# Two instead of three pairs of split buffers for the weight tiles of the feed-forwards

## The chip, the cores and the metric

The kernel runs on one core of one Trainium2 chip. The metric is the device time of one execution in microseconds (us). TensorE (PE) multiplies, VectorE (DVE) and ScalarE (ACT) work on tiles in the on-chip memory, GpSimd (POOL) and SyncE (SP) issue DMAs here.

## The reference

One decoder block on x of 256 tokens by 2048, in float32, depth 1:

```python
x = x + 0.5 * swiglu_ffn(rms_norm(x, ffn1_norm), ffn1_w_gate, ffn1_w_up, ffn1_w_down)
z = rms_norm(x, mix_norm) @ w_in                  # 2048 -> 5120
...                                               # conv, gated recurrence, short conv: y
x = x + y @ w_out                                 # 2048 -> 2048
x = x + 0.5 * swiglu_ffn(rms_norm(x, ffn2_norm), ffn2_w_gate, ffn2_w_up, ffn2_w_down)
return rms_norm(x, final_norm)

def swiglu_ffn(x, w_gate, w_up, w_down):          # 2048 -> 5632 -> 2048
    return (jax.nn.silu(x @ w_gate) * (x @ w_up)) @ w_down
```

## The kernel before

Every large product is done with operands split into two parts: `hi` is the value rounded to the type fp32r, and `lo` is what is left of it. A product is then three matmuls: weight `hi` with the activations' `hi`, weight `hi` with the activations' `lo`, weight `lo` with the activations' `hi`. The activations are split once; the weights are split as they arrive. A weight tile is 512 rows by 512 columns (`[128, UK=4, CW=512]`, 8 KB in each partition): SP fetches it into a raw buffer, ACT casts it to `hi` in two halves (`parts_of`, lines 214 to 219), DVE subtracts to get `lo` (`low_part`), and TensorE reads both. One weight tile against one group of 128 tokens is 12 matmuls of 512 columns (8 with `hi`, 4 with `lo`); against both groups, 24.

The buffers for `hi` and `lo` come from `split_tiles` (lines 198 to 206). The pool `splits`, open for the whole program, has two pairs. While `extra` holds a pool, each third weight tile takes its pair from elsewhere: in the mixer (`extra[0] is bigs`) from the pool of large tiles, otherwise from the stage's own pool, with one more pair. `extra` is set by `more_from` in `ffn` (line 526, both feed-forwards), in the mixer's `sc_c` (line 1181) and ahead of the output projection (line 1258). Outside of these, in the mixer's `columns` above all, there are two pairs.

A large part of the work goes through `seven` (lines 417 to 522): two by two blocks of a product done with seven multiplications instead of eight (a Strassen scheme), where some weight tiles are sums of others, formed in place on DVE, or by an accumulating DMA of POOL. Its order for a gate or up block is, by call:

- `product_of(0)` (raw tile w11), then DVE sums w12 into w11
- `product_of(4)` (that sum); ACT copies both results out of the accumulators (`s1`, `s5`)
- `usual(0, b2, 1)`: a plain weight tile against both token groups
- the next sum into w11, `product_of(5)`, copy `u2`
- `usual(1, b3, 1)`; `product_of(6)` (w12 with the DMA's sum), copy `u3`; `product_of(2)`
- `usual(0, a2, 0)`; a third sum; `product_of(3)`; `usual(1, a3, 0)`; `product_of(1)`

A `product_of` is 12 matmuls, a `usual` is 24. `done` adds the copies together with small DVE operations. A feed-forward (`ffn`, lines 524 to 921) begins with one column block done plainly, then has five steps `s`, each a gate block, an up block and, for `s` of 0, 2 and 4, a part of the down projection (`down`): a plain product (`product`), a block of seven, a plain product. `settle` turns finished hidden tiles with TensorE transposes (`ph`), which ACT and DVE split.

The order of the instructions on each engine is not that of the code, except in the opening of the first feed-forward, where `Engine.pinned` keeps it: a list scheduler plans it when the program is built, by its own estimate of when each operand and each buffer is ready. On the chip every engine then keeps to its planned order, and waits on semaphores. Which buffer of a pool a tile gets is decided there too. Almost all instructions have line 43 in the profile, that of the wrapper `Engine`, so groups are told apart by their tiles.

In the profile's names, `hi_g_p`, `hi_u_p`, `hi_d_p` are the tiles of a `product_of` of a gate, up or down block, `hi_g_x` those of a `usual`, `hi_d`, `hi_in` and so on those of a plain product; `ps_u_a` is the accumulator `a` of an up block, `z`, `s_g`, `s_u`, `u_g` are small result tiles.

Of the kernel before, what the change touches and what calls it, by code (L numbers as in the profile page):

```python
# [49 lines left out]
def hybrid_block(ctx: ExitStack, tc: tile.TileContext, a: dict, out: bass.AP):  # L50
# [28 lines left out]
    bigs = ctx.enter_context(tc.tile_pool(name="bigs", bufs=10, side="left"))  # L79
# [92 lines left out]
    def big(name):  # L172

        return bigs.tile([P, UK, 2 * S], F32R, tag="big", name=name)
# [3 lines left out]
    extra = []  # L178
# [18 lines left out]

    def split_tiles(name):
        pool, bufs = splits, 2
        if extra:  # L200
            turn_of["split"] += 1
            if turn_of["split"] % 3 == 0:
                if extra[0] is bigs:
                    return [big(f"{part}_{name}") for part in ("hi", "lo")]
                pool, bufs = extra[0], 1
        return [pool.tile([P, UK, CW], F32R, tag=part, name=f"{part}_{name}", bufs=bufs) for part in ("hi", "lo")]
# [7 lines left out]
    def parts_of(raw, name):  # L214
        hi, lo = split_tiles(name)
        for h in (slice(0, 2), slice(2, UK)):
            act.copy(hi[:, h, :], raw[:, h, :])
        low_part(raw, hi, lo)
        return blocks(hi, lo)
# [197 lines left out]
    def seven(w, rows, cols, sf, xs, name, keep, done, between=None, early=False, own=None, factor=None):  # L417
# [51 lines left out]
        if early:  # L469
            between("second product")  # L470
            hi, lo = split_tiles(f"{name}_x01")
            act.copy(hi, b2)
            s1 = snap(a, "s1")
            dve.tensor_tensor(w11, w22, w11, op=ALU.add)
            low_part(b2, hi, lo)
            blk = blocks(hi, lo)
        else:
            s1 = snap(a, "s1")
# [12 lines left out]
        if early:  # L491
            blk = parts_of(b3, f"{name}_x11")
            hi2, lo2 = split_tiles(f"{name}_p2")
            act.copy(hi2, w22)
            blk2 = blocks(hi2, lo2)
# [909 lines left out]
```

## Time and the profile before

| | before |
|---|---|
| median of 3 runs | 1727.16 us (1727.0 to 1728.76) |
| profiled execution | 1726.91 us, its span 1725.1 us |
| granted TensorE clock, mean | 0.999 |
| PE busy | 1715.3 us (99%), 7985 matmuls |
| DVE busy | 1452.2 us (84%) |
| ACT busy | 1077.8 us (62%) |
| fetched from memory | 339.82 MB, 198 GB/s over the span |

The span is the time from the first to the last instruction. A row of the timeline has its start (us), its duration, engine, line, operation, output and inputs, and how many instructions were merged; brackets at the end give the idle time before it and what ended it. A row of the groups has the count, then busy time in us and the mean of one in ns, then the idle time before and its releasers. PE rows of 8 matmuls last 1.98 us because the end of the last overlaps with the next row.

### The profile page before, as it was taken

The numbers are of one execution on the slowest core, as the hardware profiler recorded it, in microseconds if no ns is written. First come the engines' busy times: TensorE is split into PE (matmuls) and PEld (weight loads), VectorE is DVE, ScalarE is ACT, GpSimd is POOL, SyncE is SP. The second block draws the span as 40 slices with busy tenths as digits, with TensorE's granted clock in tenths as the row PEclk, the third lists the DMA queues.
The fourth block names the chain that finished last, engine by engine and source line by source line (L and its number), as shares of the span: only waits on it lengthen the run. The fifth ranks groups of instructions, "written<-read, shape, count | busy, mean of one in ns | idle before, by whom it ended". The sixth has DMA issues, their size and how long they took to land.

```text
span 1725.1 us, 20426 instructions
## 1 busy us (share of the span) xinstructions
PE 1715.3 (99%) x7985; PEld 1432.9 (83%) x7985; DVE 1452.2 (84%) x1212; ACT 1077.8 (62%) x1406; POOL 35.3 (2%) x62
## 2 busy tenths in 40 slices
PE   9999999999999999999999999999999999999998
PEld 8888888888888888888888888888888888888886
DVE  7988889789789888787897889889788887788886
ACT  7666566656466656666965657655556664556664
POOL 0010000000000000000000000000000000000000
PEclk9999999999999999999999999999999999999999
DMA  8775777667677766655556675776777757677753
GB/s 300 225 258 174 242 234 227 214 236 233 182 238 226 227 201 219 211 160 193 175 197 205 204 251 165 228 237 224 230 227 219 244 171 243 214 225 220 254 179 128
DMA packets 178256, 372.59 MB, mean 216 GB/s; under 512 B 6132, under 2 KB 9072, under 8 KB 174448
## 3 DMA queue, kind: packets, MB, share of 16 engines
q1 hardware_dynamic: 173632, 340.81, 58.4%
q0 software_dynamic: 4352, 29.43, 8.5%
q8 instruction: 62, 1.02, 0.2%
q10 hardware_dynamic: 176, 1.06, 0.2%
q14 instruction: 34, 0.28, 0.0%
HBM read 339.82 MB, written 2.10 MB: 198 GB/s over the span
## 4 chain that ended last, share of the span: by engine, by line
PE 99%; DVE 0%; ACT 0%; DVEq 0%; issue 0%; ACTq 0%
PE ps_d L43 14%; PE ps_in L43 10%; PE ps_g_a L43 9%; PE ps_u_a L43 9%; PE ps_g_c L43 6%; PE ps_u_c L43 6%; PE ps_d_a L43 5%; PE ps_u_d L43 5%; PE ps_g_d L43 5%; PE ps_d_c L43 3%; PE ps_u_e L43 3%; PE ps_g_e L43 3%; PE ps_g L43 3%; PE ps_o L43 3%; PE ps_u L43 3%; PE ps_d_d L43 3%
## 5 line engine op out<-in xcount | busy, mean ns | idle before, releaser
L43 ACT CAST hi_g_p<-raw_g 128x1024 fp32r<-128x1024 f32 (+1 forms) x139 | 142.1, 1054 | 111.6 <-DVE raw_g L43 26.9
L43 DVE TENSOR_TENSOR lo_g_p<-raw_g,hi_g_p 128x2048 fp32r<-128x2048 f32 x70 | 159.8, 2289 | 42.3 <-ACT hi_g_p L43 41.6
L43 DVE TENSOR_TENSOR lo_u_p<-raw_u,hi_u_p 128x2048 fp32r<-128x2048 f32 x70 | 159.3, 2288 | 39.5 <-ACT hi_u_p L43 39.2
L43 ACT CAST hi_u_p<-raw_u 128x1024 fp32r<-128x1024 f32 x140 | 141.3, 1047 | 70.1 <-issue 23.1
L43 PE MATMUL ps_d<-hi_d,h 128*128 128x512 f32 x696 | 166.0, 390 | 0.0
L43 PEld LDWEIGHTS ps_d<-hi_d,h 128*128 128x128 f32 x696 | 130.0, 188 | 26.6
L43 ACT CAST hi_d<-raw_d 128x1024 fp32r<-128x1024 f32 x88 | 88.6, 1048 | 68.3 <-PE ps_u_d L43 19.9
L43 DVE TENSOR_TENSOR lo_d<-raw_d,hi_d 128x2048 fp32r<-128x2048 f32 x44 | 100.8, 2290 | 29.3 <-ACT hi_d L43 29.3
L43 PE MATMUL ps_in<-xT_nm,hi_in 128*128 128x512 f32 x512 | 122.5, 391 | 0.0
L43 ACT CAST hi_d_p<-raw_d 128x1024 fp32r<-128x1024 f32 x84 | 85.2, 1048 | 59.2 <-DVE raw_d L43 33.7
L43 PEld LDWEIGHTS ps_in<-xT_nm,hi_in 128*128 128x128 f32 x512 | 94.0, 188 | 18.8 <-ACT tha L43 0.5
L43 DVE TENSOR_TENSOR lo_d_p<-raw_d,hi_d_p 128x2048 fp32r<-128x2048 f32 x42 | 95.5, 2288 | 15.5 <-ACT hi_d_p L43 15.4
L43 ACT CAST hi_g_x<-raw_g 128x1024 fp32r<-128x1024 f32 (+1 forms) x79 | 81.2, 1058 | 42.9 <-PE ps_g_c L43 25.6
L43 ACT CAST hi_u_x<-raw_u 128x1024 fp32r<-128x1024 f32 x80 | 80.5, 1046 | 36.4 <-PE ps_u_c L43 22.1
L43 DVE TENSOR_TENSOR lo_g_x<-raw_g,hi_g_x 128x2048 fp32r<-128x2048 f32 x40 | 91.5, 2288 | 9.2 <-ACT hi_g_x L43 8.9
L43 DVE TENSOR_TENSOR lo_in<-raw_in,hi_in 128x2048 fp32r<-128x2048 f32 x32 | 73.2, 2288 | 26.7 <-ACT hi_in L43 26.3
L43 DVE TENSOR_TENSOR lo_u_x<-raw_u,hi_u_x 128x2048 fp32r<-128x2048 f32 x40 | 91.4, 2286 | 1.4 <-ACT hi_u_x L43 0.8
L43 PE MATMUL ps_d<-lo_d,h 128*128 128x512 f32 x348 | 86.2, 389 | 0.0
L43 ACT CAST hi_in<-raw_in 128x1024 fp32r<-128x1024 f32 x64 | 64.0, 1045 | 24.9 <-PE ps_in L43 15.2
L43 PEld LDWEIGHTS ps_d<-lo_d,h 128*128 128x128 f32 x348 | 65.3, 188 | 13.6
L43 DVE TENSOR_TENSOR raw_u<-raw_u,raw_u 128x2048 f32<-128x2048 f32 x30 | 68.7, 2289 | 8.5 <-DMA raw_u<-in_ffn_w_up_dram 8.1
L43 DVE TENSOR_TENSOR raw_g<-raw_g,raw_g 128x2048 f32<-128x2048 f32 x30 | 68.7, 2289 | 5.7 <-DMA raw_g<-in_ffn_w_gate_dram 5.2
(477 smaller groups left out, 3750.5 us busy)
## 6 DMA issues: line engine op xcount, KB each, us to landing
raw_d<-in_ffn_w_down_dram SPq DMA_DIRECT2D x88, 1024.0 KB, 5.2
raw_u<-in_ffn_w_up_dram SPq DMA_DIRECT2D x87, 1024.0 KB, 5.3
raw_g<-in_ffn_w_gate_dram SPq DMA_DIRECT2D x86, 1024.0 KB, 5.2
raw_in<-in_w_in_dram SPq DMA_DIRECT2D x32, 1024.0 KB, 5.1
raw_g<-raw_g POOLq DMA_DIRECT2D x10, 1024.0 KB, 7.0
raw_u<-raw_u POOLq DMA_DIRECT2D x10, 1024.0 KB, 7.0
raw_in_c<-in_w_in_dram SPq DMA_DIRECT2D x8, 1024.0 KB, 5.3
raw_o<-in_w_out_dram SPq DMA_DIRECT2D x8, 1024.0 KB, 5.2
```

The lines of the kernel that those rows point to most:

```text
L43: ins = getattr(self.engine, name)(*args, **kwargs)
```

## The change

The condition under which `split_tiles` turns to a third pair is narrowed to the mixer's case. In the feed-forwards and in the output projection every weight tile now takes one of the two pairs of `splits`, in turn. The pair of the stage's own pool is not allocated any more, and nothing else takes its place. Arithmetic, loads and their number stay; the scheduler plans the orders anew.

```diff
     def split_tiles(name):
         pool, bufs = splits, 2
-        if extra:
+        if extra and extra[0] is bigs:
             turn_of["split"] += 1
             if turn_of["split"] % 3 == 0:
                 if extra[0] is bigs:
                     return [big(f"{part}_{name}") for part in ("hi", "lo")]
                 pool, bufs = extra[0], 1
         return [pool.tile([P, UK, CW], F32R, tag=part, name=f"{part}_{name}", bufs=bufs) for part in ("hi", "lo")]
```

## The prediction, made before the changed kernel had run

> **What bounds the kernel now.** I read the page first: busy shares and the chain that ended last.
>
> ```profile
> span 1725.1 us, 20426 instructions
> ...
> PE 1715.3 (99%) x7985; PEld 1432.9 (83%) x7985; DVE 1452.2 (84%) x1212; ACT 1077.8 (62%) x1406; POOL 35.3 (2%) x62
> ...
> PE 99%; DVE 0%; ACT 0%; DVEq 0%; issue 0%; ACTq 0%
> ```
>
> TensorE is busy 99% of the span and is the whole chain. Second view, what TensorE waits for: one row that names a split tile.
>
> ```profile
> PE ps_g L43 <- ACT hi_g L43: 0.6, 1, 0.6
> ```
>
> So the splits (ScalarE casts the high part, VectorE subtracts the low part) have always been ready. Nothing can be won: the idle time of TensorE is 1725.1 - 1715.3 = 9.8 us, and its instructions stay the same. Everything turns on whether the splits stay ahead with two pairs. Third view, the groups: what a split costs.
>
> ```profile
> L43 DVE TENSOR_TENSOR lo_u_p<-raw_u,hi_u_p 128x2048 fp32r<-128x2048 f32 x70 | 159.3, 2288 | 39.5 <-ACT hi_u_p L43 39.2
> L43 ACT CAST hi_u_p<-raw_u 128x1024 fp32r<-128x1024 f32 x140 | 141.3, 1047 | 70.1 <-issue 23.1 <-PE ps_u_a L43 22.6 <-DVE raw_u L43 22.0
> 322.00:364.00 42.00, 42.00 (x191) 34.85 (x190) 34.62 (x22) 26.96 (x31) 0.87 (x1) 1.00 0.73 236
> ```
>
> A low part is 2.29 us, a high part two casts of 1.05 us. The last row (busy time by stretch: PE, PEld, DVE, ACT, POOL, granted clock) is an up-projection's seven-product block: VectorE is busy 34.6 of 42 us, so it has capacity; what it may lack is look-ahead.
>
> **One seam, instruction by instruction.** The timeline where a gate block ends and an up block begins, by engine. I name a weight tile after its call: P0 is product_of(0), X01 is usual(0, b2, 1), X10 is usual(1, a3, 0). A P tile has 12 matmuls, an X tile 24. The PE rows are, in order: P3 (2 rows), X10 (4), P1 (2, of which the first is shown), then in the up block P0 (2), P4, X01, P5, X11.
>
> ```profile
> 313.70 1.98 PE L43 MATMUL ps_g_a<-hi_g_p,x 128*128 128x512 f32 x8
> 315.51 1.07 PE L43 MATMUL ps_g_a<-lo_g_p,x 128*128 128x512 f32 x4
> 316.42 1.98 PE L43 MATMUL ps_g_a<-hi_g_x,x 128*128 128x512 f32 x8
> 318.23 1.98 PE L43 MATMUL ps_g_d<-hi_g_x,x 128*128 128x512 f32 x8
> 320.05 1.07 PE L43 MATMUL ps_g_a<-lo_g_x,x 128*128 128x512 f32 x4
> 320.95 1.07 PE L43 MATMUL ps_g_d<-lo_g_x,x 128*128 128x512 f32 x4
> 321.86 1.98 PE L43 MATMUL ps_g_d<-hi_g_p,x 128*128 128x512 f32 x8
> ...
> 324.58 1.98 PE L43 MATMUL ps_u_a<-hi_u_p,x 128*128 128x512 f32 x8
> 326.39 1.07 PE L43 MATMUL ps_u_a<-lo_u_p,x 128*128 128x512 f32 x4
> 327.30 1.98 PE L43 MATMUL ps_u_c<-hi_u_p,xs 128*128 128x512 f32 x8
> ...
> 330.02 1.98 PE L43 MATMUL ps_u_e<-hi_u_x,x 128*128 128x512 f32 x8
> ...
> 335.46 1.98 PE L43 MATMUL ps_u_a<-hi_u_p,xs 128*128 128x512 f32 x8
> ...
> 338.18 1.98 PE L43 MATMUL ps_u_e<-hi_u_x,x 128*128 128x512 f32 x8
> ```
>
> ```profile
> 315.75 2.00 ACT L43 CAST hi_u_p<-raw_u 128x1024 fp32r<-128x1024 f32 x2 [1.63 <-issue]
> 321.15 0.60 ACT L43 ACTIVATE z<-ps_g_a 128x512 f32<-128x512 f32 x1 [3.40 <-PE ps_g_a L43]
> 322.49 2.00 ACT L43 CAST hi_u_p<-raw_u 128x1024 fp32r<-128x1024 f32 x2 [0.74 <-DVE raw_u L43]
> ...
> 327.99 0.58 ACT L43 ACTIVATE s_u<-ps_u_a 128x512 f32<-128x512 f32 x1
> 330.22 0.60 ACT L43 ACTIVATE s_u<-ps_u_c 128x512 f32<-128x512 f32 x1 [1.65 <-PE ps_u_c L43]
> ```
>
> ```profile
> 317.79 2.29 DVE L43 TENSOR_TENSOR lo_u_p<-raw_u,hi_u_p 128x2048 fp32r<-128x2048 f32 x1 [1.34 <-ACT hi_u_p L43]
> 320.11 2.29 DVE L43 TENSOR_TENSOR raw_u<-raw_u,raw_u 128x2048 f32<-128x2048 f32 x1
> 324.52 2.29 DVE L43 TENSOR_TENSOR lo_u_p<-raw_u,hi_u_p 128x2048 fp32r<-128x2048 f32 x1 [2.12 <-ACT hi_u_p L43]
> 326.74 0.68 DVE L43 TENSOR_TENSOR s_g<-ps_g_d,s_g 128x512 f32<-128x512 f32 x1
> ```
>
> Read what starts P0's high part, at 315.75. The profile says "issue", so no wait that it sees; but P3's high part was last read by the matmuls that end where the next PE row begins, at 315.51, and 0.24 us later the cast starts. P3 lies three tiles before P0 (P3, X10, P1, P0): the cast waits for the third pair to come round. The rest hangs on it: P0's low part 317.79, then VectorE forms the sum w11 + w12 in place (320.11), which is P4's raw tile, then P4's high part (322.49 to 324.49) and low part (324.52 to 326.81). TensorE asks for P4 at 327.30: the lead is 2.8 us for the high part.
>
> PE rows give matmuls 0.227 us apart (8 in 1.81 us), and the other latencies: a cast ends at 317.75 and its subtraction starts at 317.79 (0.04); a sum ends at 322.40 and its cast starts at 322.49 (0.09); X10's matmuls into ps_g_a end where the next row begins, 320.95, and z starts 0.20 later. Operations that follow each other on ACT start 0.1 us before the one before them has ended.
>
> **With two pairs, step by step.** Now P0 takes the pair of the tile two before it, X10. I walk on in the same times, with the orders of the changed program. Two things in them differ at this seam: ACT issues z between the two halves of P0's high part, and s_g's and s_u's activations ahead of P4's high part; VectorE adds s_g ahead of the sum.
>
> X10's high part is free at 320.05 + 0.20 = 320.25 and its low part at 321.86 + 0.20 = 322.06. High part of P0: first half 320.25 to 321.3, z to 321.8, second half to 322.8. Low part 322.8 to 325.1. s_g's small add, then the sum from 325.6 to 327.9. ACT has s_u, the copy of the finished P0 product: it can't start before 327.30 + 0.20 and ends at 328.1, and P4's cast stands behind it. First half of P4's high part 328.0 to 329.05. TensorE wanted it at 327.30 and gets it at 329.1: **a wait of 1.8 us where there was none.** From there: the second half ends at 330.0, P4's low part 330.05 to 332.35; the new PE order puts 6 of X01's high matmuls ahead of P4's low ones, which covers this: with X01's first half at 330.95 they run from 331.0 to 332.4, 0.15 us lost. P4's low matmuls end at 333.3; the copy of ps_u_c (0.60 us, the row at 330.22) holds X01's second target until 334.15, where 8 matmuls covered it before and 2 do now: 0.4 us lost. VectorE does X01's low part to 334.6 and the next sum to 336.8; P5's first half is there at 337.95, and TensorE, which has done X01 at 337.75, loses 0.25 us. X11's first half comes at 339.85 and costs 0.1 us. P5's low part (338.9 to 341.2) is again covered by 6 matmuls of X11. At 342.2 TensorE has 10 of X11's 16 high matmuls left; before, it was there at 338.18 + 6 x 0.227 = 339.54. Loss 2.65 us. Later in the block the tiles are longer or need no sum; P3's low part comes just in time behind five small adds (0 to 0.5 us). I take **2.9 us a seam**.
>
> Bounds: at least 0.9 us, if nothing on ACT stands in the way of P0 and P4 (low part at 322.06, sum to 327.1, half a cast later 328.2 against 327.30); at most 4.0 us, with P3's 0.5 and another 0.1 us on each of some six crossings.
>
> Loads: the walk delays the release of raw tiles, so fetches start later. A fetch takes 5.3 us to land:
>
> ```profile
> raw_u<-in_ffn_w_up_dram SPq DMA_DIRECT2D x87, 1024.0 KB, 5.3
> ```
>
> The nearest is w21, fetched after X11's low part (about 343.6, so there at 349) for a sum that VectorE reaches at about 349: just hidden. I take nothing; if the cover fails it is part of the 4.0.
>
> **How many seams.** The bad place is P1, P0, P4 in a row: short tiles, with a sum between the last two. It exists where a block follows a block: all five up blocks of both feed-forwards (10), and gate blocks 2 and 4 (4), which follow up blocks. The changed PE order says the same: in those 14 blocks X01's high matmuls were moved ahead of P4's low ones. In the gate seam 8 transposes stand ahead of P1 and their copies on ACT; the same walk gives about 3. 14 x 2.9 = 41 us.
>
> The other blocks of seven (gate 1 and 3, gate 0, three down blocks, per feed-forward, and the one of the output projection: 13) come after plain products, whose rows are these:
>
> ```profile
> 430.37 21.76 PE ps_d L43 x96
> ```
>
> Each plain tile is 24 matmuls, 5.44 us, against 2.29 us of VectorE: P0's low part can start a whole plain tile ahead of P0, and P4 is in time. Inside, P5, P6, P2 can cost 0 to 1.5 us; I take 0.6, 8 us in all (0 to 20). Plain products, the mixer's columns (which never had the third pair) and the tail: nothing, each tile has 9 us for its low part. The two openings: 0 to 2 us each, I take 1 each.
>
> **Sum.** 41 + 8 + 2 = 51 us. The profiled execution took 1726.9 us (its span 1725.1 and 1.8 around it), 0.25 below the median shown, 1727.16. Predicted 1778.
>
> A rule of the Trainium skill speaks of the first wait. "TensorE: Matmul & The Clock Gate", Part 1, says that TensorE's clock is halved after an idle window of about 3.4 us. By it my longest wait, 1.8 us, is too short, and the sum stays; the profile's granted clock is 1.00 in the stretch quoted above, and no row of it shows what a wait does.
>
> **Rivals.**
>
> *No wait appears (not slower).* Place: P4 of each of the 14 seams. The moved matmuls of the next X tile fill the time, and two pairs are enough. Price 0: 1727. It decides if P0's low part starts 1.8 us sooner than I have it, at 321.0. For it: VectorE has 7 us free in 42. Against: X10's low matmuls are only then being read (320.05 to 321.86). "Trainium Kernel Development and Optimization", Best Practices, asks for double buffering for performance and no more; that is this rival. Chance 0.05, of which faster by chance of the new order 0.02.
>
> *Shorter.* ACT's order doesn't bite and only the 0.9 us and the small waits after it stay, 1.2 a seam, with 5 for the rest: 14 x 1.2 + 5 = 22, 1749. Against: an engine's own order is fixed in the program. Chance 0.12.
>
> *Wider.* Every one of the 27 blocks pays 2.9, since P5, P6, P2 is the same pattern as P1, P0, P4: 27 x 2.9 = 78, 1805. Against: there TensorE comes out of a 24-matmul tile. Chance 0.12.
>
> *The clock falls.* If a wait drops the granted clock to half for as long as one plain tile, each of 14 seams pays 5.44 us more: 1778 + 76 = 1854. No row shows the clock below 1.00. Chance 0.03.
>
> **How the numbers follow.** My forecast has 0.68. The bounds, 14 x 0.9 with nothing else and 14 x 4.0 + 20 + 4, give 1740 to 1807; the range 1750 to 1808 takes the upper bound in, with the wider rival, and leaves out the clock, no wait, and half of the shorter one and the bottom of the bounds: about 0.2. A measurement here can tell about 0.2% (3.5 us). Faster 0.02, same 0.03, slower 0.95.
>
> **What the profile after would show.** Right: TensorE's busy time as before or stretched, with gaps of 1 to 2 us ahead of P4 in the 14 seams; P0's cast starting 0.2 us after X10's high matmuls; a period of 44 us instead of 41 to 42 for an up block; ACT's s_u ahead of P4's cast. Plain products unchanged. The prediction is wrong if the gaps lie mostly elsewhere (P5, P6, the openings), if the granted clock is below 0.99, or if the span grows by less than 13 us or more than 80.

## The result, and the profile after

| | before | after |
|---|---|---|
| median | 1727.85 us (4 runs, 1727.0 to 1728.76) | 1779.31 us (4 runs, 1777.98 to 1779.55) |
| profiled span | 1725.1 us | 1777.6 us |
| granted TensorE clock, mean | 0.999 | 0.999 |

The ratio is 1.0296, with a 95% interval of 1.0278 to 1.0314: the changed kernel is 3% slower. The forecast was 1778.0 us (1750 to 1808). The page of the kernel after (span, busy times, chain that ended last, and one group of the splits):

```profile
span 1777.6 us, 20462 instructions
...
PE 1735.6 (98%) x7985; PEld 1425.6 (80%) x7985; DVE 1451.0 (82%) x1212; ACT 1078.5 (61%) x1406; POOL 35.5 (2%) x62
...
PE 92%; DVE 3%; ACT 3%; issue 1%; DMA 1%; DVEq 0%; ACTq 0%
...
L43 DVE TENSOR_TENSOR lo_u_p<-raw_u,hi_u_p 128x2048 fp32r<-128x2048 f32 x70 | 160.3, 2290 | 84.4 <-ACT hi_u_p L43 82.3
```

No engine has more work: the 7985 matmuls, the 1212 operations of VectorE and the 1406 of ScalarE are those of before, and a subtraction still takes 2.29 us. What is new is that VectorE and ScalarE stand in the chain (3% each), and that VectorE's idle time before `lo_u_p`, nearly all for the high part, has gone from 39.5 to 84.4 us. The waits of TensorE name the place (total, times, longest):

```profile
PE ps_u_c L43 <- ACT hi_u_p L43: 16.2, 10, 1.6
PE ps_g_c L43 <- ACT hi_g_p L43: 7.3, 5, 1.6
PE ps_d_d L43 <- DVE lo_d_x L43: 2.4, 2, 1.2
PE ps_u_c L43 <- ACT s_u L43: 2.0, 9, 0.2
```

`ps_u_c` and `ps_g_c` with a `hi` of a P tile are P4 of an up and of a gate block: 10 up blocks and 5 gate blocks wait there. Among them is each of the 14 seams of the prediction; the fifteenth is gate block 0 of the second feed-forward.

The rows show 32.2 us of the 52.5 us as idle (1777.6 - 1735.6 = 42.0, against 9.8 before); the other 20.3 us count as busy. Matmuls have not become slower, but for a few at the start of the program. A group that never waits has the same mean as before, here in the groups after:

```profile
L43 PE MATMUL ps_u_a<-hi_u_p,x 128*128 128x512 f32 x160 | 39.5, 389 | 0.0
```

One matmul's row lasts 0.389 us and the next starts 0.227 us after it, so 0.16 us of each lies under the next row, and where TensorE has to wait, that end stands out and is counted as work. The wait at P4, 1.62 us of idle time in the row below, is 1.78 us from start to start. So I add up losses by starts of rows, block by block.

The same seam as in the prediction (end of a gate block, up block), from the timeline after, TensorE: X10's low part, P1's first row, P0 (2 rows), P4's high part, then X01 and P4's low part interleaved, and the start of P5.

```profile
334.69 1.07 PE L43 MATMUL ps_g_a<-lo_g_x,x 128*128 128x512 f32 x4
...
336.51 1.98 PE L43 MATMUL ps_g_d<-hi_g_p,x 128*128 128x512 f32 x8
...
339.23 1.98 PE L43 MATMUL ps_u_a<-hi_u_p,x 128*128 128x512 f32 x8
341.04 1.07 PE L43 MATMUL ps_u_a<-lo_u_p,x 128*128 128x512 f32 x4
343.73 2.15 PE L43 MATMUL ps_u_c<-hi_u_p,xs 128*128 128x512 f32 x8 [1.62 <-ACT hi_u_p L43]
345.71 1.59 PE L43 MATMUL ps_u_e<-hi_u_x,x 128*128 128x512 f32 x6
347.14 1.09 PE L43 MATMUL ps_u_c<-lo_u_p,xs 128*128 128x512 f32 x4
348.06 0.63 PE L43 MATMUL ps_u_e<-hi_u_x,x 128*128 128x512 f32 x2
348.91 2.09 PE L43 MATMUL ps_u_c<-hi_u_x,x 128*128 128x512 f32 x8 [0.22 <-ACT s_u L43]
...
352.66 2.03 PE L43 MATMUL ps_u_a<-hi_u_p,xs 128*128 128x512 f32 x8
```

```profile
334.89 1.05 ACT L43 CAST hi_u_p<-raw_u 128x1024 fp32r<-128x1024 f32 x1 [2.53 <-PE ps_g_d L43]
335.85 0.59 ACT L43 ACTIVATE z<-ps_g_a 128x512 f32<-128x512 f32 x1
336.34 1.04 ACT L43 CAST hi_u_p<-raw_u 128x1024 fp32r<-128x1024 f32 x1
...
342.14 0.60 ACT L43 ACTIVATE s_u<-ps_u_a 128x512 f32<-128x512 f32 x1 [1.18 <-PE ps_u_a L43]
342.64 1.98 ACT L43 CAST hi_u_p<-raw_u 128x1024 fp32r<-128x1024 f32 x2
344.52 2.00 ACT L43 CAST hi_u_x<-raw_u 128x1024 fp32r<-128x1024 f32 x2
```

```profile
337.41 2.29 DVE L43 TENSOR_TENSOR lo_u_p<-raw_u,hi_u_p 128x2048 fp32r<-128x2048 f32 x1 [2.72 <-ACT hi_u_p L43]
339.62 0.68 DVE L43 TENSOR_TENSOR s_g<-ps_g_d,s_g 128x512 f32<-128x512 f32 x1
340.22 2.28 DVE L43 TENSOR_TENSOR raw_u<-raw_u,raw_u 128x2048 f32<-128x2048 f32 x1
```

Read the chain. ScalarE stands idle for 2.53 us and casts P0's high part at 334.89, when X10's last matmuls that read its high part have ended (334.69 + 0.20); the profile now names TensorE as what released it, where before it said "issue". Then z between the two halves, P0's low part at 337.41, s_g, the in-place sum at 340.22 to 342.50. TensorE has done P0 by 341.95, ScalarE copies its result (s_u) at 342.14 and casts P4 right behind it at 342.64, and TensorE starts P4 at 343.73.

### The profile page after: what moved, and what is told of

It reads as the page before. It is cut to its first block, busy times and chain, and to the rows that moved or that the text cites. A ratio compares the mean times of both kernels' runs of the same rounds, so it can differ in the third digit from the quotient of the medians.

```text
span 1777.6 us, 20462 instructions
## 1 busy us (share of the span) xinstructions
PE 1735.6 (98%) x7985; PEld 1425.6 (80%) x7985; DVE 1451.0 (82%) x1212; ACT 1078.5 (61%) x1406; POOL 35.5 (2%) x62
## 4 chain that ended last, share of the span: by engine, by line
PE 92%; DVE 3%; ACT 3%; issue 1%; DMA 1%; DVEq 0%; ACTq 0%
PE ps_d L43 13%; PE ps_in L43 10%; PE ps_u_a L43 9%; PE ps_g_a L43 9%; PE ps_u_c L43 7%; PE ps_g_c L43 5%; PE ps_u_d L43 5%; PE ps_g_d L43 5%; PE ps_d_a L43 4%; PE ps_g_e L43 3%; PE ps_u_e L43 3%; PE ps_o L43 2%; PE ps_d_c L43 2%; PE ps_d_d L43 2%; PE ps_g L43 2%; PE ps_u L43 2%
## 5 line engine op out<-in xcount | busy, mean ns | idle before, releaser
L43 DVE TENSOR_TENSOR lo_u_p<-raw_u,hi_u_p 128x2048 fp32r<-128x2048 f32 x70 | 160.3, 2290 | 84.4 <-ACT hi_u_p L43 82.3
```

What stands on the lines that cost most here:

```text
L43: ins = getattr(self.engine, name)(*args, **kwargs)
```

## The experiments

Every experiment but the last starts from the changed kernel. Ratios are to the kernel before, with 95% intervals.

**The third pair for P0 alone.** In `split_tiles`, behind the line that the change left:

```diff
         pool, bufs = splits, 2
+        if extra and extra[0] is not bigs and name.endswith("_p0"):
+            pool, bufs = extra[0], 1
```

> Two pairs for every tile, and the third pair for the P0 tile of each block of seven alone (one weight tile in eleven). Theory (look-ahead at the seam: P0's cast waits for X10's pair, and the in-place sum and P4 hang on it): the 1.78 us wait ahead of P4 goes in all 14 seams, with the small waits that follow it; what is left are the other blocks and the openings, so 1728 to 1744, likeliest 1737. Rival (the third pair helps evenly, each tile that has it a little): a tile in eleven instead of one in three brings back at most a third of the 52 us, 1762 or more.

Measured: 1731.17 us (8 runs), 1.0019 [1.0009, 1.0030]. In its timeline, VectorE, ScalarE and TensorE at the same seam:

```profile
314.77 2.28 DVE L43 TENSOR_TENSOR lo_u_p<-raw_u,hi_u_p 128x2048 fp32r<-128x2048 f32 x1
...
321.72 2.29 DVE L43 TENSOR_TENSOR raw_u<-raw_u,raw_u 128x2048 f32<-128x2048 f32 x1
...
324.10 2.00 ACT L43 CAST hi_u_p<-raw_u 128x1024 fp32r<-128x1024 f32 x2 [0.58 <-DVE raw_u L43]
...
329.07 1.98 PE L43 MATMUL ps_u_c<-hi_u_p,xs 128*128 128x512 f32 x8
```

P0's low part is begun 14 us ahead of P4's matmuls, and P4's cast begins 5 us ahead of them. P4 waits in none of the 14 seams. One pair, used by one tile of each block of seven, gives back 48 of the 51 us. So the loss hangs on when P0's pair comes free.

**The third pair for another tile, X00.** The same edit with `_x00` in place of `_p0`.

> The counterpart: the third pair for the X00 tile of each block of seven alone, as many tiles as P0. Theory: the seam still runs in two pairs, P4's wait stays at 1.6 to 1.8 us in 14 seams, 1772 to 1781, likeliest 1777. Rival (even help): the same time as with the third pair on P0.

Measured: 1769.58 us (2 runs), 1.0238 [1.0218, 1.0259], 2.4 us below the range. The waits of TensorE at P4 are to the digit those of the changed kernel:

```profile
PE ps_u_c L43 <- ACT hi_u_p L43: 16.2, 10, 1.6
PE ps_g_c L43 <- ACT hi_g_p L43: 7.3, 5, 1.6
```

The 14 seams still lose 2.65 to 2.75 us each. The 10 us gained lie elsewhere, and I had not expected them: the two waits of `ps_d_d` for `lo_d_x` are gone (the first down block of each feed-forward loses 0.09 instead of 2.28 us), and the rest comes in small pieces (1.2 us of it in the first opening, where it is not the pairs' doing, as shown further down). A third pair helped in both places tried, by 48 us at P0 and by 10 at X00.

**The sum in a buffer of its own.** Two pairs, but the first sum of a block, P4's raw tile, no longer goes over w11, the raw tile of P0. So it needn't wait for P0's low part to be read from there. It takes one buffer of 8 KB per partition where the third pair takes 16.

```diff
         product_of(0, w11, a, True)
-        dve.tensor_tensor(w11, w12, w11, op=ALU.add)
+        total = w11 if early or extra[0] is bigs else extra[0].tile([P, UK, CW], F32, tag="sum", name=f"sum_{name}", bufs=1)
+        dve.tensor_tensor(total, w12, w11, op=ALU.add)
+        w11 = total
```

> Two pairs, but the first sum w11 + w12 of a feed-forward or output block goes into a buffer of its own (8 KB in each partition) instead of into w11, except in the pinned first block. It then needn't wait for P0's low part. Theory (it is the chain P0's high part, low part, in-place sum, P4's high part that turns a late pair into a wait): P4's high part can start at the release of P1's high part, 3 us ahead of its use, and the wait goes although P0 still gets its pair late: 1732 to 1745, likeliest 1738. Rival (TensorE is short of pairs as such, P0 or P4 would wait for a buffer whatever the sum does): 1770 or more.

Measured: 1732.09 us (10 runs), 1.0024 [1.0014, 1.0033]. Its timeline, VectorE, ScalarE, TensorE:

```profile
316.55 2.29 DVE L43 TENSOR_TENSOR sum_u<-raw_u,raw_u 128x2048 f32<-128x2048 f32 x1
...
323.93 1.05 ACT L43 CAST hi_u_p<-raw_u 128x1024 fp32r<-128x1024 f32 x1 [2.54 <-PE ps_g_d L43]
...
327.56 2.00 ACT L43 CAST hi_u_p<-sum_u 128x1024 fp32r<-128x1024 f32 x2 [1.15 <-PE ps_g_d L43]
...
330.99 1.29 PE L43 MATMUL ps_u_c<-hi_u_p,xs 128*128 128x512 f32 x5
```

P0's cast is still as late as in the changed kernel: it waits 2.5 us for TensorE, as there. But the sum was begun 7.4 us before it and done 5.1 us before it (318.84), and P4's cast waits only for its own buffer. The wait at P4 is gone in all 14 seams with only two pairs. So the late pair does harm through one chain: P0's cast, P0's low part, the sum over the same buffer, P4's cast.

**A third buffer for the high part only, then for the low part only.** `split_tiles` gives each third weight tile a `hi` (or a `lo`) from the stage's pool, and everything else from the two pairs:

```diff
-        return [pool.tile([P, UK, CW], F32R, tag=part, name=f"{part}_{name}", bufs=bufs) for part in ("hi", "lo")]
+        where = {"hi": pool, "lo": pool}
+        if extra and extra[0] is not bigs:
+            turn_of["split"] += 1
+            if turn_of["split"] % 3 == 0:
+                where["hi"] = extra[0]
+        return [
+            where[part].tile([P, UK, CW], F32R, tag=part, name=f"{part}_{name}", bufs=2 if where[part] is splits else 1)
+            for part in ("hi", "lo")
+        ]
```

> Every third tile of the feed-forwards and the output projection takes its high part from a third buffer, all low parts share two. Theory: P0's high part is early again, but its low part can start only when X10's low part has been read, 0.2 us after P1 begins; the sum then ends about 1.3 us earlier than with two pairs and P4 waits 0.4 to 0.6 us: 1740 to 1758, likeliest 1748. Rival (the halves of the pair count alike): half of the 52 us, about 1753, and the same with the low part alone tripled.

> Every third tile takes its low part from a third buffer, all high parts share two. Theory: P0's low part waits for its high part anyway (second half cast at 322.8 in the times of the kernel before, the buffer free at 322.06), so nothing is gained at the seam: P4's wait stays at 1.6 to 1.8 us, 1772 to 1781, likeliest 1777. Rival (the halves count alike): about 1753.

Measured, high part: 1767.04 us (2 runs), 1.0223 [1.0203, 1.0244], 9 us above the range. Measured, low part: 1777.43 us (2 runs), 1.0287 [1.0266, 1.0307], where expected, with the two rows of waits at P4 unchanged (16.2 and 7.3 us). So of the two buffers it is the high part's that is late; but with it freed the gain is 12 us, not 31. The timeline and the waits of TensorE with the third high part:

```profile
338.09 1.20 PE L43 MATMUL ps_u_c<-hi_u_p,xs 128*128 128x512 f32 x4 [0.41 <-ACT hi_u_p L43]
...
341.88 1.20 PE L43 MATMUL ps_u_c<-lo_u_p,xs 128*128 128x512 f32 x4
343.76 2.11 PE L43 MATMUL ps_u_c<-hi_u_x,x 128*128 128x512 f32 x8 [0.69 <-ACT s_u L43]
...
348.01 2.14 PE L43 MATMUL ps_u_a<-hi_u_p,xs 128*128 128x512 f32 x8 [0.32 <-ACT hi_u_p L43]
```

```profile
PE ps_u_c L43 <- ACT hi_u_p L43: 5.4, 14, 0.5
PE ps_u_c L43 <- ACT s_u L43: 4.5, 8, 0.7
```

P4's first wait fell from 1.78 to 0.57 us (start to start), as this experiment supposed. What I missed is that in the up blocks most of the 1.2 us turn up again a few tiles on: the copy of `ps_u_c` out of the accumulator costs 0.97 us (341.88 + 4 x 0.227 to 343.76) instead of 0.40, and P5 now waits 0.48 us. Seven of the ten up blocks still lose 2.6 to 2.7 us, the others 1.3, 2.2 and 3.5. At the four gate seams the gain stays: they lose 0.9 us each instead of 2.7 to 3.0.

**An own high buffer for P0 alone, low parts in the two pairs.** The same edit as for `hi`, with the condition `name.endswith("_p0")`. It makes true one part of the condition under which the prediction put its lower bound, 0.9 us a seam: P0's cast is out of the way, but what else ScalarE has to do around P4 stays.

> Two pairs, and a buffer of its own for the high part of P0 alone. The study with a third high buffer in the ring gained at P4 (0.57 us instead of 1.78) but paid in the up blocks behind it. Theory A (paid because other tiles' casts ran ahead of P4's and P5's on ACT, which the ring of three high buffers allowed): here no other tile gains a buffer, so the up blocks lose about 1.2 us a seam and the time is 1745 to 1762. Theory B (P4's early start only moves the wait to the copy of ps_u_c and to P5, whoever has the buffer): up blocks lose 2.4 to 2.7 us again, 1764 to 1772.

Measured: 1767.13 us (2 runs), 1.0225 [1.0203, 1.0247]. The time is that of theory B, 1764 to 1772. Timeline, TensorE, ScalarE and VectorE:

```profile
336.95 1.19 PE L43 MATMUL ps_u_c<-hi_u_p,xs 128*128 128x512 f32 x4 [0.41 <-ACT hi_u_p L43]
338.42 1.20 PE L43 MATMUL ps_u_c<-hi_u_p,xs 128*128 128x512 f32 x4 [0.28 <-ACT hi_u_p L43]
339.85 1.21 PE L43 MATMUL ps_u_e<-hi_u_x,x 128*128 128x512 f32 x4 [0.23 <-ACT hi_u_x L43]
```

```profile
335.85 1.05 ACT L43 CAST hi_u_p<-raw_u 128x1024 fp32r<-128x1024 f32 x1 [5.02 <-DVE raw_u L43]
336.80 0.63 ACT L43 ACTIVATE s_g<-s_g 128x512 f32<-128x512 f32 x1
337.33 1.03 ACT L43 CAST hi_u_p<-raw_u 128x1024 fp32r<-128x1024 f32 x1
338.27 0.59 ACT L43 ACTIVATE s_u<-ps_u_a 128x512 f32<-128x512 f32 x1
338.76 1.98 ACT L43 CAST hi_u_x<-raw_u 128x1024 fp32r<-128x1024 f32 x2
```

```profile
331.14 2.29 DVE L43 TENSOR_TENSOR lo_u_p<-raw_u,hi_u_p 128x2048 fp32r<-128x2048 f32 x1 [2.03 <-PE ps_g_d L43]
```

One wait of 1.78 us has become three, of 0.57, 0.44 and 0.39 us from start to start. The first is still the sum's: P0's low part can begin only at 331.14, when TensorE has read X10's low part. The other two are the order on ScalarE: s_g stands between the halves of P4, s_u between P4 and X01, and each pushes a half cast behind the matmuls that want it. So the wait did move on, as theory B has it, but to P4's second half and to X01, and not to the copy of `ps_u_c` and P5. An up block loses 2.25 to 2.54 us in eight of ten cases (1.95 and 3.20 in the others), a gate seam 1.5. So freeing P0's high part brings the first wait below the 0.9 us of the bound, and still not the seam.

**P0's high part in one cast.** If z stood between the halves at a cost, one cast of the whole tile would take it out:

```diff
-        for h in (slice(0, 2), slice(2, UK)):
+        for h in (slice(0, UK),) if name.endswith("_p0") and extra[0] is not bigs else (slice(0, 2), slice(2, UK)):
```

> Two pairs; P0's high part is one cast of the whole tile instead of two halves, so z can't come between them on ACT. Theory: P0's low part starts 0.6 us earlier, and the sum then goes ahead of s_g's small add, another 0.6 us: P4's wait falls from 1.78 to about 0.6 us. 14 x 1.2 = 17 us less, 1758 to 1772, likeliest 1763. Rival (ACT's order costs nothing, only the buffers count): 1777 to 1781.

Measured: 1770.56 us (4 runs), 1.0244 [1.0227, 1.0261], inside the range, at its upper end. Waits of TensorE:

```profile
PE ps_u_c L43 <- ACT hi_u_p L43: 8.3, 20, 0.6
PE ps_u_c L43 <- DVE lo_u_p L43: 3.7, 7, 1.8
```

The waits for `hi_u_p` are half as long in total as in the changed kernel (8.3 us against 16.2) and twice as many, and a new wait for a low part appears. P4's first wait in the up blocks fell from 1.78 to 0.72 us, near the 0.6 expected; but of the 9 us that come back, only 1.6 are in the ten up blocks, where z had stood between the halves, against 4.5 in the four gate seams. In one of these (P4 at 299.00 in the changed kernel) nothing had stood between P0's halves: they were cast at 289.27 in 2.00 us. So taking z out brought little back, and the gain at the gate seams comes from something else that the new plan changed; what it was stays open.

**A long tile last, with two pairs.** P1 (12 matmuls) and X10 (24) change places at the end of a gate or up block, so that X10 lies between P1, whose pair P0 now takes, and P0. No buffer is added.

```diff
+        swap = two and not own and extra[0] is not bigs
+        if swap:
+            product_of(1, w21, d, False, False)
         if two:
-            usual(1, a3, 0, (a, 1, False, True), (d, 0, False, False))
+            usual(1, a3, 0, (a, 1, False, True), (d, 0, False, swap))
         done(1, 0, a, [])
-        product_of(1, w21, d, own is not None)
+        if not swap:
+            product_of(1, w21, d, own is not None)
```

> Two pairs everywhere, no buffer added; in the gate and up blocks and the down blocks with a second plain tile, the last two products change places: P1 comes ahead of X10, so a block ends on a tile of 24 matmuls and the next block's P0 takes P1's pair, free a whole long tile ahead. Theory (the seam stalls because three short tiles meet there): P0's low part ends 2.9 us ahead of P0, P4's high part is in time, what is left at a seam is 0 to 0.5 us: 1733 to 1755, likeliest 1745. Rival (two pairs are too few for this VectorE load wherever the short tiles lie): the wait moves to another tile, 1770 or more.

The same exchange was made in the kernel before, to see what the order costs with three pairs.

> The kernel before, three pairs, with the same exchange of the last two products. Theory: TensorE never waited there, so nothing is to be won: 1725 to 1731. Rival (the order of the products has a price or a gain of its own, which the two-pair version would share): more than 4 us off the kernel before.

Measured, from the changed kernel: 1751.13 us (4 runs), 1.0132 [1.0114, 1.0150]; from the kernel before: 1729.12 us (10 runs), 1.0002 [0.9993, 1.0012]. Both are inside their ranges. With three pairs the order is worth nothing; with two it gives back 28 us. Timeline of the former, ScalarE and then TensorE (P0, P4):

```profile
327.20 2.00 ACT L43 CAST hi_u_p<-raw_u 128x1024 fp32r<-128x1024 f32 x2 [0.72 <-PE ps_g_d L43]
```

```profile
335.16 1.07 PE L43 MATMUL ps_u_a<-lo_u_p,x 128*128 128x512 f32 x4
336.06 1.98 PE L43 MATMUL ps_u_c<-hi_u_p,xs 128*128 128x512 f32 x8
```

P0's cast again waits for a pair to come free, but P4's matmuls are now wanted 8.9 us after it (327.20 to 336.06), where in the changed kernel they were wanted 7.1 us after it (334.89 to 341.95) and came after 8.8. P4 follows P0 with no wait. Nine of the ten up blocks lose 0.34 to 0.77 us, a little more than the 0 to 0.5 expected, the tenth 1.43. Of the 24 us that its span is still longer, the 14 seams take about 9 and the first down blocks of the two feed-forwards 6.4 (3.98 and 2.39, in part at `ps_d_d` as in the changed kernel); the rest is spread over the other blocks.

## Why the prediction was right

It was right in its mechanism, and close in most sizes, some of them by luck. Its walk went in the times of the kernel before; the seam quoted above lies 14.65 us later (P1's first row, 336.51 against 321.86), so 14.65 is taken off.

| step | predicted | measured |
|---|---|---|
| P0's cast starts | 320.25 | 320.24 |
| P0's low part starts | 322.8 | 322.76 |
| the sum starts | 325.6 | 325.57 |
| P4's cast starts | 328.0 | 327.99 |
| wait ahead of P4 | 1.8 us | 1.78 us, in all 14 seams |
| X01's first half late | 0.15 us | 0.17 us, but in P4's own matmuls |
| copy of `ps_u_c` holds X01's second target | 0.4 us | 0.40 us |
| X01's six matmuls ahead of P4's low part | nothing | 0.07 us |
| first matmuls behind the copy | nothing | 0.12 us |
| P5's first half | 0.25 us | 0.0 us |
| P5's second half and X11 | 0.1 us | 0.12 us |

**The seam.** 2.9 us were taken; the 14 seams lost 2.65 to 3.73, together 39.7 us (2.84 each) against 41. In the seam shown the measured column adds up to 2.66 us, where the walk had 2.65. That the two agree so well is partly luck, and so is the mean. The 0.17 us were spent between P4's first matmul and X01's (343.73 to 345.71, 1.98 us instead of 1.81), most of it in the first matmul behind the wait; X01's first half, cast by 345.57, was then in time. P5's 0.25 us was wrong: TensorE, late by another 0.19 us around P4's low part and the copy, reached P5 at 338.01 in those times, not at 337.75, and its high part was there; the same lateness was met once and not twice. The 0.25 us that were added to the walk, for P3's low part, did not come in this seam, nor in ten others, which lost 2.65 to 2.75 us. Three seams lost 3.0 to 3.7 and lift the mean; in two of them P3's low part is late, by about 0.4 and 0.8 us, once more than the 0.5 allowed for.

**What stood ahead of P4's cast.** The prediction had ScalarE's copy s_u ahead of it, and that is the limit, by little. The cast starts 0.49 us after s_u does (342.14 and 342.64), as a half cast does after z (335.85 and 336.34); by the sum alone, which ends at 342.50, it could have begun at 342.59, with the 0.09 us from a sum to its cast. So the sum is 0.05 us short of being the limit in the up blocks. At the four gate seams the copy of P0's result (there s_g) stands in the same place and the sum ends 0.32 us ahead of the cast, 0.23 us earlier than it would have to. This is why the wait is 1.78 us in all 14 seams, although the work ahead of the sum differs between up and gate blocks: it is 0.20 us from the end of P0's matmuls to the copy, 0.49 to the cast, 1.09 to P4's first matmul. By the sum alone it would have been about 1.73 us in the up blocks and 1.55 in the gate seams. The late sum is thus the cause of nearly all of the wait, and the planned order on ScalarE of the last 0.05 to 0.23 us. No run moved the copy alone: in the three kernels without the wait the plan also put s_u behind P4's cast. The lower bound of 0.9 us a seam assumed a clear ScalarE; with P0's high part freed, the up blocks lost 1.3 to 3.5 us, and only the four gate seams with a third high buffer came down to it.

**The other blocks.** 8 us for 13 blocks; they lost 10.8. The term was an even 0.6 us, and the loss isn't even: four blocks lost under 0.2 us, but the first down block of each feed-forward 2.28 us, where `ps_d_d` waits 1.36 us (start to start) for the low part of an X tile, a place that the prediction didn't look at, and gate block 0 of the second feed-forward lost 1.78. Openings: 2.0 us against 2, by luck. 1.8 us of them lie in the first feed-forward's opening, and are not the pairs' doing: the first matmuls of its first product start about 0.43 us apart (5.88 to 8.61 us), against 0.23 in the kernel before, and the trace's record of the granted clock has full speed from 9.7 us on, against 4.8. The kernel with the long tile last has the same two pairs, full speed from 6.0 us on, and loses 0.03 us there. The second opening lost 0.3. Plain products and the mixer's columns: 0.0, as said. 39.7 + 10.8 + 2.0 = 52.5, the difference of the spans.

**The rivals.** No wait: every seam shows one. Shorter, 1.2 us a seam: no seam of the changed kernel lost less than 2.65. Wider, 2.9 us in all 27 blocks: the other 13 lost 0.8 on average. The clock: 0.999 on average, as before. "TensorE: Matmul & The Clock Gate", Part 1, of the Trainium skill has the clock halved after an idle window of about 3.4 us; the longest wait here, 1.78 us, left the mean granted clock where it was in all 14 places, which agrees; no run here has one near 3.4 us in mid-kernel. "Trainium Kernel Development and Optimization", Best Practices, of the Trainium skill asks for double buffering, to overlap DMA with compute; taken for the split buffers too, as the first rival took it, it costs 51 us in this kernel, and 4 us where the sum has its own buffer.

**What the experiments' own forecasts missed.** The chain is shown: three different cuts of it (P0's pair, the sum's buffer, a long tile between) take the wait away. Where it was only loosened, I had expected the whole gain of the first wait, 31 us for the third high buffer and 16 for the one cast, and found 12 and 9. In the up blocks most of the wait moved to the next half tiles behind, in ScalarE's planned order; in the gate seams much of the gain stayed. In these kernels the scheduler planned every engine anew, so how much of the new waits is the hardware's need and how much the plan's choice stays open; the same work in another fixed order was not tried.

## What to carry to other kernels

Two pairs of buffers between the splitting engines and TensorE would have been enough here if, at the worst place, the work that TensorE does between the release of a buffer and the use of what depends on it had been longer than the chain in between. Count that chain through in-place operations too. In the seam shown TensorE has 32 matmuls, from 334.69 to 341.95 (7.26 us). The chain of two half casts with z between them, a subtraction, a small add, a sum and half a cast takes 8.99 us by its rows, and with the copy s_u just ahead of the last cast 9.04 us, from 334.69 to 343.73, although VectorE was busy for only 82% of the time; the difference of 1.78 us is the wait. When memory is short, look for the one tile that needs the depth, for the in-place write that ties two tiles together, or for a longer tile to put last. A chain that was only shortened handed most of its wait on in the up blocks of three runs here, so add up the whole block and not the first wait.

## What the runs showed of the hardware that I had not expected

The waits repeat almost to the digit. P4 waits 1.78 us in all 14 seams of the kernel after, though loads, other blocks and the mixer lie between them, and rows of 16.2 and 7.3 us came out the same in three different kernels. In this case four starts along the chain could be worked out to 0.04 us from rows of another kernel; the whole loss of a seam could not, it went from 2.65 to 3.73 us.

After a wait TensorE lost a little more than the wait: the first matmul behind P4's wait (343.73) and the first behind the copy's (348.91) took 0.34 us to the next one instead of 0.227, with no wait that the profile names.
